# First and last RMS norm with one sum per token column, squares shared with VectorE, and the first weight group split inside that chain

## The chip, the cores and the metric

The kernel runs on one core of a Trainium2 chip. A time is the device time of one execution in microseconds (us). The engines are TensorE (PE, with its weight loads shown apart as PEld), VectorE (DVE), ScalarE (ACT), GpSimd (POOL) and SyncE (SP, which here only starts transfers). The kernel before takes 947.25 us, the median of three runs from 946.94 to 947.63.

## The reference

One trunk layer of a hybrid diffusion backbone runs on 128 context tokens and 512 latent tokens with 1024 features, in float32. What matters here are its first and last steps:

```
def rmsnorm(x, g):
    xf = x.astype(jnp.float32)
    y = xf * lax.rsqrt(jnp.mean(xf * xf, axis=-1, keepdims=True) + EPS)
    return y.astype(x.dtype) * g

h = rmsnorm(x, p['norm1_g']) * (1 + sc1) + sh1          # sub-layer 1, then the big input projection
proj = jnp.einsum('btd,dc->btc', h, p['w_in']) + p['b_in']
...                                                      # mLSTM, convolution, merge, gated MLP
y_prompt = rmsnorm(xc, final_norm_g)                     # last step
y_sample = rmsnorm(xl, final_norm_g)
```

The shift and scale (sh1, sc1) come from SiLU of a conditioning vector times a 1024 x 6144 matrix. The mLSTM, the two convolutions, the merge and the MLP between the first and the last norm are not touched by the change.

## The kernel before

Activations lie with features on the 128 partitions and the 640 tokens (128 context, 512 latent) along the columns, so x is eight tiles of 128 x 640. Every large product is made from three float32r products of a high and a low part: a weight group `wst` of eight 128 x 128 blocks is loaded, ScalarE copies it to the high part `wh`, and VectorE subtracts to get the low part `wl` (or a transfer adds it). The activations are split likewise into `hh` and `hl`.

The order of the work on each engine is the order in which the program issues it. A small planner (`_Order`) keeps an estimate of each engine's time; generators given to `od.spawn` are resumed when the estimate says that what they need is there (`od.until`), so filler work is woven into the matmul stream. It decides order only; on the chip, semaphores decide when something starts. `od.force` runs one such generator to its end at once.

**The start (lines 704 to 830).** SP starts the transfers of x[0..3], `cols` (the small per-feature constants), x[4..7], `sel` (which holds the identity `ident` and selection columns), then the conditioning matrix tiles `adst` and the first weight groups. For each x[j], ScalarE squares it (`sq`), and `colsum_into` adds it up on TensorE: four matmuls with 32 columns of ones as stationary operand, in the four column groups of the array, each streaming a quarter of the tokens (160 columns); the sums of eight tiles accumulate in one PSUM bank as 4 x 160 values, each repeated over 32 partitions. After x[3], ScalarE computes a Tanh of the conditioning vector and loads the Sqrt table. `rstd` turns the 160-column sums into the reciprocal root: a Sqrt on ScalarE, then on VectorE a scale, a reciprocal and one Newton step (three more instructions), each 160 columns wide. `bcast` spreads the result over all partitions in token order with four matmuls of 160 columns, and ScalarE copies it to `rbs`. The generator `ada1` makes the modulation: per tile j, eight float32 matmuls on `adst` (16 passes in the trace), a ScalarE copy `mrow`, two matmuls on `mrow`, then two small VectorE instructions for `mods` and `a`. `first_h(j)` multiplies x[j] by the spread factor, and makes hh and hl. Then the first projections start. A float32 matmul shows in the trace as two passes, each with its own weight load.

**The end (lines 1742 to 1790).** The last down-projections go in two token parts: `dnA` for the first TL = 384 tokens and `dnB` for the other 256. For each feature tile the residual is added on VectorE, ScalarE squares it, and VectorE adds up the squares of tiles 0 to 6 (`square_sum`); tile 7 stays apart, so there are two sums. `final(h)` then calls `sums_in` (which calls `colsum_into` twice), `rstd`, `bcast_part` (four matmuls) and the final multiply on VectorE, with a transfer out. The first part's final multiplies are woven between the second part's residuals. The middle norm uses the same helpers and keeps them.

Of the kernel before, what the change touches and what calls it, by code (L numbers as in the profile page):

```python
# [12 lines left out]
AF = mybir.ActivationFunctionType  # L13
ALU = mybir.AluOpType

P = 128
D = 1024
KD = D // P
NCTX = 128
NLAT = 512  # L20
T = NCTX + NLAT
TH = T // 2
NH = 4
NCH = T // P
# [52 lines left out]
TL = 384  # L77
# [281 lines left out]
def tile_trunk(  # L359
# [17 lines left out]
    od = _Order()  # L377
    V, S, G, PE, Q, GQ = (_Timed(e, od, k) for e, k in ((nc.vector, "V"), (nc.scalar, "S"), (nc.gpsimd, "G"),
                                                        (nc.tensor, "PE"), (nc.sync, "Q"), (nc.gpsimd, "R")))
# [19 lines left out]
    first, last = ExitStack(), ctx.enter_context(ExitStack())  # L399
    adp = first.enter_context(tc.tile_pool(name="adp", bufs=2 * NAD1))  # L400

    def A(shape, dt=F32, name="a"):
        return ap.tile(shape, dt, tag="A", name=name)
# [18 lines left out]
    def ps():  # L422
        return od.ring("ps", pools["ps"].tile([P, 512], F32, tag="ps", name="ps"), pools["nps"])
# [2 lines left out]
        return t[:, 0:T].rearrange("p (h n) -> p h n", h=2)  # L426

    HALF = [slice(0, TH), slice(TH, T)]


    cols = cp.tile([P, NCOLS], F32, name="cols")
    sel = cp.tile([P, NSEL], F32, name="sel")
    ident = sel[:, 0:128]
# [15 lines left out]
    lines = {}  # L449
# [5 lines left out]
    def load(g, must=True):  # L455
        if g in stage or g in ready or g in raws or g >= NGRP:
            return
        while len(live) >= NST:
            if not must:
                return  # L460
            od.force(next(t for t in lines.values() if not t[2]))
        t = od.ring("st", sp.tile([P, GB * P], F32, tag="st", name="wst"), NST)
        Q.dma_start(t, w_d[g])
        stage[g] = t
        live[g] = len(READS[g not in PAIRS]) if g in PAIRS or g - 1 in PAIRS else 1
# [1 line left out]
    def wtile(tag):  # L467
        return od.ring(tag, (wf[0] if tag == "wf" else wp).tile([P, GB * P], F32R, tag=tag, name=tag), CAPS[tag])

    def prep(g, tags=("wh", "wl")):  # L470


        if g in ready or g >= NGRP:
            return
        load(g)
        src = stage.pop(g)
        tag_of["c", g, 0] = tags
        hi, lo = wtile(tags[0]), wtile(tags[1])

        def parts():  # L480
            yield from od.until(src)
            S.activation(hi, src, AF.Copy)
            if g in TWICE:
                S.activation(lo, src, AF.Copy, scale=-1.0)
                live.pop(g)
                GQ.dma_start(lo, w_d[g], accum_op=ALU.add)
                return
            yield
            V.tensor_sub(lo, src, hi.bitcast(F32))
            live.pop(g)  # L490

        ready[g] = (hi, lo)
        lines[g] = od.spawn(parts())
# [137 lines left out]
    def mtile(mat, m, ks, xs, pt=None, first=True, last=True):  # L631
        pt = mm_ps() if pt is None else pt
        outs = [(bank(pt, h), HALF[h]) for h in range(2)]
        for i, k in enumerate(ks):
# [3 lines left out]
    def views(pt, t, rows=slice(0, P)):  # L638
# [3 lines left out]
        if isinstance(pt, tuple):  # L642
            return [(bank(pt, h)[rows], t[:, HALF[h]]) for h in range(2)]
        return [(pt[rows, :, 0:TH], halves(t))]
# [10 lines left out]
    ones32 = cp.tile([P, 32], F32, name="ones32")  # L655
    V.memset(ones32, 1.0)
    epsc = cp.tile([P, 1], F32, name="epsc")
    V.memset(epsc, EPS)
    bgrp = T // 4

    def colsum_into(pc, tile_, n, first, last):
        for g in range(4):
            PE.matmul(pc[32 * g:32 * g + 32, 0:n], lhsT=ones32, rhs=tile_[:, g * n:(g + 1) * n],
                      start=first, stop=last, tile_position=(0, 32 * g))

    def bcast(r, n):
        out = []
        for h in range(2):
            pt = ps()
            for j in range(2):  # L670
                g = 2 * h + j
                PE.matmul(pt[:, j * n:(j + 1) * n], lhsT=sel[:, 256 + g:257 + g].to_broadcast([P, P]), rhs=r,
                          start=True, stop=True)
            out.append(pt[:, 0:2 * n])
        return out

    def rstd(src, w, scale, name):

        y = small([P, w], name + "y")
        S.activation(y, src, AF.Sqrt, scale=scale, bias=epsc)  # L680
        v = small([P, w], name + "v")
        V.tensor_scalar(v, src, scale, EPS, op0=ALU.mult, op1=ALU.add)
        V.reciprocal(y, y)
        t = small([P, w], name + "t")
        V.tensor_mul(t, y, y)
        V.scalar_tensor_tensor(t, t, -0.5, v, op0=ALU.mult, op1=ALU.mult)
        V.scalar_tensor_tensor(y, t, 1.5, y, op0=ALU.add, op1=ALU.mult)
        return y
# [7 lines left out]
    x = []  # L696
    for j in range(KD):
        t = A([P, T], name="x")
# [21 lines left out]
    pc = ps()  # L720
    for j in range(KD):
        sq = A([P, T], name="sq")
        S.activation(sq, x[j], AF.Square)
        if j == 3:
            th = small([P, 16], "th")
            S.activation(th, colr("c"), AF.Tanh, scale=0.5)
            sqrt_table()
        colsum_into(pc, sq, bgrp, j == 0, j == KD - 1)
    V.scalar_tensor_tensor(th, th, 1.0, colr("c"), op0=ALU.add, op1=ALU.mult)
    sc_pad = cp.tile([P, KD, 32], F32, name="sc_pad")  # L730
    V.memset(sc_pad, 0.0)
# [8 lines left out]
    for nm in ("b_ua", "b_ub", "b_o", "mlstm_g", "ln_g", "ln_b", "b_ga", "b_gb"):  # L740
        a, b = _COLS[nm]
# [1 line left out]
        HC[nm] = o  # L743
        o += b - a

    r1 = rstd(pc[:, 0:bgrp], bgrp, 1.0 / D, "rs")
    prep(0)

    def hcol(name, i):
        return halfc[:, HC[name] + i:HC[name] + i + 1]  # L750
# [31 lines left out]
    def first_h(j):  # L782
        while not rbs:
            yield
        if j == 0:
            for h in range(2):
                V.tensor_mul(x[j][:, HALF[h]], x[j][:, HALF[h]], rb[h])
        else:
            V.tensor_mul(x[j], x[j], rbs[0])
        hh, hl = A([P, T], F32R, "hh"), A([P, T], F32R, "hl")  # L790
        hs.append((hh, hl))
        yield
        for c, s in ((0, slice(0, NCTX)), (1, slice(NCTX, T))):
            S.activation(hh[:, s], x[j][:, s], AF.Identity, scale=a1[:, j, c:c + 1], bias=mods[:, j, c:c + 1])
        for c, s in ((0, slice(0, NCTX)), (1, slice(NCTX, T))):
            V.tensor_scalar(x[j][:, s], x[j][:, s], a1[:, j, c:c + 1], mods[:, j, c:c + 1], op0=ALU.mult, op1=ALU.add)
        V.tensor_sub(hl, x[j], hh.bitcast(F32))
# [4 lines left out]
    t_ada = od.spawn(ada1())  # L802
    while not mrows:
        od.finish_one()
    rb = bcast(r1, bgrp)
    t = A([P, T], name="rbs")
    for h in range(2):
        S.activation(t[:, HALF[h]], rb[h], AF.Copy)
    rbs.append(t)
    pu = [mm_ps(), mm_ps()]  # L810
    pl = [ps()[:, 0:T - NFST] for _ in range(2)]
# [128 lines left out]
    for p in range(2):  # L940
        for c in range(NCH):
            t = vp.tile([P, 2, P1], F32, tag="v", name="va")
# [437 lines left out]
    for i, (nm, m) in enumerate(BRANCH):  # L1380
# [9 lines left out]
        else:  # L1390
# [4 lines left out]
            a, b = sgt.pop(("ga", m)), sgt.pop(("gb", m))  # L1395
# [33 lines left out]
    def sums_in(sums, adds, n):  # L1429

        while not all(t[2] for t in adds):
            yield
        pc = ps()
        for i in range(2):
            yield from od.until(sums[i])
            colsum_into(pc, sums[i], n, i == 0, i == 1)
        return pc[:, 0:n]

    def bcast_part(r):
        pt = ps()  # L1440
        n = r.shape[1]
        for g in range(4):
            PE.matmul(pt[:, g * n:(g + 1) * n], lhsT=sel[:, 256 + g:257 + g].to_broadcast([P, P]), rhs=r,
                      start=True, stop=True)
        return pt[:, 0:4 * n]
# [35 lines left out]
    def norm2_part(h, j, rb):  # L1481
        s = HALF[h]
        t, hh = hf[j][:, h, :], h2[j, h]
# [38 lines left out]
    for h in range(2):  # L1522
        sums, adds = [], []
        mat, s = ("woA", "woB")[h], HALF[h]
        pts = [mhalf(mat, m, range(KD - 1), mg, s, last=False) for m in range(2 if h == 0 else 0)]
        for m in range(8):
            if m < len(pts):
                pt = mhalf(mat, m, [KD - 1], mg[KD - 1:], s, pt=pts[m], first=False)
            else:
                pt = mhalf(mat, m, range(KD), mg, s)  # L1530
# [6 lines left out]
    for i in range(2):  # L1537
        t = A([P, TF], name=f"gbuf{i}")
# [200 lines left out]

    ks = LASTF  # L1740

    PARTS = [slice(0, TL), slice(TL, T)]

    def final(h, sums, adds):
        s = PARTS[h]
        n = (s.stop - s.start) // 4
        pc = yield from sums_in(sums, adds, n)
        r3 = rstd(pc, n, 1.0 / D, "rs")
        yield
        yield from od.until(r3)  # L1750
        rb = bcast_part(r3)
        if h == 0:
            for j in range(KD):
                V.scalar_tensor_tensor(x2[j][:, s], x2[j][:, s], col("final_g", j), rb, op0=ALU.mult, op1=ALU.mult)
                Q.dma_start(yT[j, :, s], x2[j][:, s])
                yield
            return
        for j in range(0, KD, 2):
            t = A([P, 2, 4 * n], name="yo")
            for i in range(2):  # L1760
                V.scalar_tensor_tensor(t[:, i, :], x2[j + i][:, s], col("final_g", j + i), rb,
                                       op0=ALU.mult, op1=ALU.mult)
            Q.dma_start(yT[j:j + 2, :, s].rearrange("j p n -> p j n"), t)
# [3 lines left out]
    for h in range(2):  # L1767
        mat, s = ("dnA", "dnB")[h], PARTS[h]
        sums, adds = [], []
        npre = NPRE if h == 0 else 0  # L1770
        pts = [dn(mhalf, mat, m, ks[:-1], s, last=False) for m in range(npre)]
        for m in range(8):
# [3 lines left out]
            if m < npre:  # L1776
                pt = dn(mhalf, mat, m, ks[-1:], s, pt=pts[m], first=False)
            else:
                pt = dn(mhalf, mat, m, ks, s)
# [136 lines left out]
```

## Time and profile before

| what | value |
| --- | --- |
| median of 3 runs (lowest, highest) | 947.25 us (946.94, 947.63) |
| the profiled execution: its time, its span | 948.37 us, 946.6 us |
| PE busy in the span | 914.1 us (97%) |
| DVE busy, ACT busy, POOL busy | 755.4 us (80%), 521.2 us (55%), 130.0 us (14%) |
| mean granted TensorE clock | 0.992 |
| chain that ended last, by engine | PE 84%, DVE 8%, ACT 4%, DMA 2%, issue 2% |

The span runs from the first to the last instruction; the execution's own time is 1.77 us longer, for what lies around it. A busy share is an average over the whole span: it says that TensorE is the engine to watch, not which engine sets the pace in the first 22 us or the last 12, where the change lies. The chain that ended last says that: it is followed back from the last instruction through whatever released each step.

### The profile page before, as it was taken

The numbers are of one execution on the slowest core, as the hardware profiler recorded it, in microseconds if no ns is written. First come the engines' busy times: TensorE is split into PE (matmuls) and PEld (weight loads), VectorE is DVE, ScalarE is ACT, GpSimd is POOL, SyncE is SP. The second block draws the span as 40 slices with busy tenths as digits, with TensorE's granted clock in tenths as the row PEclk, the third lists the DMA queues.
The fourth block names the chain that finished last, engine by engine and source line by source line (L and its number), as shares of the span: only waits on it lengthen the run. The fifth ranks groups of instructions, "written<-read, shape, count | busy, mean of one in ns | idle before, by whom it ended". The sixth has DMA issues, their size and how long they took to land.

```text
span 946.6 us, 16998 instructions
## 1 busy us (share of the span) xinstructions
PE 914.1 (97%) x6456; PEld 892.1 (94%) x6456; DVE 755.4 (80%) x1541; ACT 521.2 (55%) x994; POOL 130.0 (14%) x180
## 2 busy tenths in 40 slices
PE   5999999999999999999999989999999999999995
PEld 2899999999999999999998989999999999999995
DVE  3838989998897888888788996777778877878666
ACT  5562564267644523224689836656765666666662
POOL 0100201000000000000004313222222222222210
PEclk9999999999999999999999999999999999999998
DMA  9624939211342355576458959787888888889875
GB/s 354 263 101 80 223 79 216 73 41 61 90 134 87 126 167 200 180 268 200 155 167 186 242 152 216 166 182 165 184 170 179 177 179 176 180 177 182 205 168 150
DMA packets 65810, 158.61 MB, mean 168 GB/s; under 512 B 6848, under 2 KB 17856, under 8 KB 65728
## 3 DMA queue, kind: packets, MB, share of 16 engines
q1 hardware_dynamic: 41360, 113.20, 36.9%
q0 software_dynamic: 24368, 44.31, 28.2%
q8 instruction: 51, 0.84, 0.4%
q14 instruction: 31, 0.25, 0.1%
HBM read 142.48 MB, written 3.48 MB: 154 GB/s over the span
## 4 chain that ended last, share of the span: by engine, by line
PE 84%; DVE 8%; ACT 4%; DMA 2%; issue 2%; POOL 0%; SPq 0%; DVEq 0%; POOLq 0%; ACTq 0%
PE mm L178 64%; PE ps L178 19%; DVE acc L178 1%; DVE z L178 1%; DMA wst<-in_w 1%; DVE wl L178 1%; ACT wh L178 1%; DMA x<-in_xT 1%; DVE junk L178 1%; DMA wf<-sf 1%; DVE x L178 1%; ACT hf L178 0%; ACT L178 0%; DVE hf L178 0%; DVE bc L178 0%
## 5 line engine op out<-in xcount | busy, mean ns | idle before, releaser
L178 ACT ACTIVATE wh<-wst 128x1024 fp32r<-128x1024 f32 (+1 forms) x114 | 113.9, 1006 | 96.5 <-PE mm L178 81.9
L178 DVE SCALAR_TENSOR_TENSOR acc<-gbuf,cols,acc 128x455 f32<-128x455 f32 (+2 forms) x176 | 129.6, 739 | 16.5 <-ACT acc L178 14.0
L178 PE MATMUL mm<-hh,wh 128*128 128x320 f32 (+2 forms) x576 | 133.9, 311 | 2.5 <-ACT hh L178 1.6
L178 PE MATMUL mm<-hh,wl 128*128 128x320 f32 (+2 forms) x576 | 134.0, 312 | 0.2 <-DVE wl L178 0.2
L178 PE MATMUL mm<-hl,wh 128*128 128x320 f32 (+2 forms) x576 | 133.3, 310 | 0.0
L178 DVE SCALAR_TENSOR_TENSOR z<-glu,cols,z 128x641 f32<-128x641 f32 (+14 forms) x120 | 102.4, 888 | 6.3 <-ACT z L178 5.5
L178 DVE TENSOR_TENSOR wl<-wst,wh 128x1024 fp32r<-128x1024 f32 x72 | 87.6, 1220 | 19.7 <-ACT wh L178 19.3
L178 PEld LDWEIGHTS mm<-hh,wh 128*128 128x128 f32 x576 | 96.7, 188 | 4.6 <-ACT hh L178 2.1
L178 PEld LDWEIGHTS mm<-hl,wh 128*128 128x128 f32 x576 | 96.5, 188 | 1.8 <-issue 1.3
L178 PEld LDWEIGHTS mm<-hh,wl 128*128 128x128 f32 x576 | 96.3, 188 | 1.4 <-issue 0.7
L178 PE MATMUL mm<-h,wh 128*128 128x320 f32 x452 | 85.7, 310 | 2.3 <-ACT h L178 1.3
L178 PE MATMUL mm<-ah,wh 128*128 128x320 f32 (+2 forms) x336 | 81.1, 311 | 5.2 <-DVE x L178 5.2
L178 DVE SCALAR_TENSOR_TENSOR junk<-ad,cb 128x512 bf16<-128x512 f32 x128 | 82.1, 685 | 0.0
L178 PE MATMUL mm<-al,wh 128*128 128x320 f32 (+2 forms) x336 | 80.9, 310 | 0.0
L178 PE MATMUL mm<-ah,wl 128*128 128x320 f32 (+2 forms) x336 | 80.8, 310 | 0.0
L178 PEld LDWEIGHTS mm<-h,wh 128*128 128x128 f32 x452 | 71.1, 188 | 4.0 <-ACT h L178 1.6
L178 PE MATMUL mm<-h,wl 128*128 128x320 f32 x364 | 73.1, 309 | 0.0
L178 DVE SCALAR_TENSOR_TENSOR x<-mm,mods,x 128x128 f32<-128x128 f32 (+1 forms) x168 | 63.7, 432 | 7.2 <-PE mm L178 6.6
L178 POOL DMA_DIRECT2D wl<-in_w x52 | 45.1, 868 | 144.1 <-ACT wl L178 65.9
L178 PEld LDWEIGHTS mm<-ah,wh 128*128 128x128 f32 x336 | 57.7, 189 | 5.6 <-issue 5.4
L178 ACT ACTIVATE wl<-wst 128x512 fp32r<-128x512 f32 (+1 forms) x74 | 56.4, 792 | 4.7 <-PE mm L178 4.7
L178 PEld LDWEIGHTS mm<-h,wl 128*128 128x128 f32 x364 | 58.4, 188 | 0.1
(250 smaller groups left out, 1944.6 us busy)
## 6 DMA issues: line engine op xcount, KB each, us to landing
wst<-in_w SPq DMA_DIRECT2D x138, 512.0 KB, 4.5
ad<-in_ada SPq DMA_DIRECT2D x64, 256.0 KB, 3.3
wl<-in_w POOLq DMA_DIRECT2D x30, 512.0 KB, 7.4
adst<-in_ada SPq DMA_DIRECT2D x16, 512.0 KB, 10.2
wf<-in_w POOLq DMA_DIRECT2D x23, 256.0 KB, 5.4
wh<-sf POOLq DMA_DIRECT2D x22, 256.0 KB, 5.1
wl<-in_w POOLq DMA_DIRECT2D x22, 256.0 KB, 6.1
x<-in_xT SPq DMA_DIRECT2D x16, 320.0 KB, 5.2
```

The lines of the kernel that those rows point to most:

```text
L178: return fn(*args, **kw)
```

## The change

Both outer norms take their sums in another shape. In `token_sums` the squared tile is the stationary operand (128 tokens at a time) and one column of ones is streamed, so that the sum of token p of chunk c lands on partition p, column c: five matmuls of one column for 640 tokens. `rstd` then works on 5 columns at the start, and on 3 and 2 at the end. `token_rows` spreads the result: the column of a chunk, repeated 128 times, is the stationary operand and the identity is streamed. In the start, VectorE squares x[3], x[4], x[5] and x[7], the Tanh and the Sqrt table follow x[2], and the first weight group is split right after the first `mrow`, ahead of the spread, without the planner's wait for its landing. The first norm's parts are now 384 and 256 tokens instead of 320 and 320. The new functions are whole in the diff.

```
-    def prep(g, tags=("wh", "wl")):
+    def prep(g, tags=("wh", "wl"), wait=True):
...
         def parts():
-            yield from od.until(src)
+            if wait:
+                yield from od.until(src)
             S.activation(hi, src, AF.Copy)
...
+    def token_sums(pc, tile_, w, first, last):
+
+        n = w // P
+        for c in range(n):
+            PE.matmul(pc[:, c:c + 1], lhsT=tile_[:, c * P:(c + 1) * P], rhs=ones32[:, 0:1], start=first and c == 0,
+                      stop=last and c == n - 1)
+
+    def token_rows(r, a, b):
+
+        pt = ps()
+        for c in range(a, b):
+            PE.matmul(pt[:, (c - a) * P:(c - a + 1) * P], lhsT=r[:, c:c + 1].to_broadcast([P, P]), rhs=ident,
+                      start=True, stop=True)
+        return pt[:, 0:(b - a) * P]
...
         sq = A([P, T], name="sq")
-        S.activation(sq, x[j], AF.Square)
-        if j == 3:
+        if j in (3, 4, 5, 7):
+            V.tensor_mul(sq, x[j], x[j])
+        else:
+            S.activation(sq, x[j], AF.Square)
+        if j == 2:
...
-        colsum_into(pc, sq, bgrp, j == 0, j == KD - 1)
+        token_sums(pc, sq, T, j == 0, j == KD - 1)
...
-    r1 = rstd(pc[:, 0:bgrp], bgrp, 1.0 / D, "rs")
-    prep(0)
+    r1 = rstd(pc[:, 0:NCH], NCH, 1.0 / D, "rs")
...
             for h in range(2):
-                V.tensor_mul(x[j][:, HALF[h]], x[j][:, HALF[h]], rb[h])
+                V.tensor_mul(x[j][:, PARTS[h]], x[j][:, PARTS[h]], rb[h])
...
-    rb = bcast(r1, bgrp)
+    prep(0, wait=False)
+    od.force(lines[0])
+    rb = [token_rows(r1, 0, 3), token_rows(r1, 3, NCH)]
...
     def final(h, sums, adds):
         s = PARTS[h]
-        n = (s.stop - s.start) // 4
-        pc = yield from sums_in(sums, adds, n)
-        r3 = rstd(pc, n, 1.0 / D, "rs")
+        n = (s.stop - s.start) // P
+        while not all(t[2] for t in adds[:-1]):
+            yield
+        yield from od.until(sums[0])
+        pc = ps()
+        token_sums(pc, sums[0], n * P, True, False)
+        while not adds[-1][2]:
+            yield
+        yield from od.until(sums[1])
+        token_sums(pc, sums[1], n * P, False, True)
+        r3 = rstd(pc[:, 0:n], n, 1.0 / D, "rs")
         yield
         yield from od.until(r3)
-        rb = bcast_part(r3)
+        rb = token_rows(r3, 0, n)
...
```

## Rows read from the trace of the kernel before

**Rows 1.** The chain that ended last, start of the kernel: start us, length us, what.

```profile
10.52 2.69 PE ps L178 x32
...
16.17 4.35 PE ps L178 x28
...
20.93 1.09 ACT hh L178 x2
...
22.06 0.56 PE mm L178 x2
```

**Rows 2.** Busy time by engine in a stretch, after the start.

```profile
22.00:40.00 18.00, 17.94 (x167) 14.13 (x168) 14.73 (x33) 8.74 (x18) 3.47 (x17) 1.00 0.89 354
```

**Rows 3.** The chain that ended last, end of the kernel.

```profile
934.89 0.41 DVE x L178
...
935.79 0.36 PE ps L178 x8
...
936.17 0.32 ACT rsy L178
...
938.13 1.96 PE ps L178 x8
```

**Rows 4.** Timeline of PE in the start: start us, us, operation.

```profile
4.35 0.76 PE L178 MATMUL ps<-sq,ones 128*32 128x160 f32 x8 [4.35 <-ACT sq L178]
...
18.46 1.01 PE L178 MATMUL ps<-sel,mrow 128*128 128x128 f32 x4
...
19.41 1.07 PE L178 MATMUL ps<-adst,sc_pad 128*32 128x256 f32 x16
...
22.46 0.61 PE L178 MATMUL ps<-sel,mrow 128*128 128x128 f32 x4
```

**Rows 5.** PE groups by form: count, busy us, mean ns of one, idle before.

```profile
L178 PE MATMUL ps<-rsy,sel 128*128 128x64 f32 x8 | 1.9, 424 | 2.0 <-DVE rsy L178 2.0
```

**Rows 6.** Issues on SP, and time to landing of x[7] and of the first wst.

```profile
3.08 2.43 SPq L178 DMA_DIRECT2D x<-in_xT  x4
...
DMA to landing us min/median/max: 6.6/6.6/6.6
...
8.10 0.33 SPq L178 DMA_DIRECT2D wst<-in_w  x1
...
DMA to landing us min/median/max: 7.4/7.4/7.4
```

**Rows 7.** Stretches after PE idled from 563.5 to 568.7; last columns: clock, DMA.

```profile
571.00:572.00 1.00, 1.00 (x6) 1.00 (x5) 0.58 (x1) 1.00 (x3) 0.04 (x1) 0.50 0.82 319
572.00:573.00 1.00, 1.00 (x8) 1.00 (x7) 0.78 (x2) 1.00 (x3) 0.83 (x1) 0.87 0.94 348
```

**Rows 8.** Timeline of DVE and ACT between the sums and the first projection.

```profile
13.90 1.14 DVE L178 RECIPROCAL rsy<-rsy 128x160 f32<-128x160 f32 x1
...
15.79 0.32 DVE L178 SCALAR_TENSOR_TENSOR rsy<-rst,rsy 128x160 f32<-128x160 f32 x1
...
19.04 1.05 ACT L178 ACTIVATE wh<-wst 128x1024 fp32r<-128x1024 f32 x1
...
19.84 0.87 DVE L178 TENSOR_TENSOR x<-x,ps 128x320 f32<-128x320 f32 x2
...
20.63 1.22 DVE L178 TENSOR_TENSOR wl<-wst,wh 128x1024 fp32r<-128x1024 f32 x1
```

**Rows 9.** Timeline of DVE in the last norm.

```profile
936.66 0.54 DVE L178 RECIPROCAL rsy<-rsy 128x64 f32<-128x64 f32 x1
...
937.76 0.23 DVE L178 SCALAR_TENSOR_TENSOR rsy<-rst,rsy 128x64 f32<-128x64 f32 x1
```

**Rows 10.** Timeline of PE near the end, first part's sums and spread, last product.

```profile
922.70 0.54 PE L178 MATMUL ps<-sq,ones 128*32 128x96 f32 x16
...
926.66 1.13 PE L178 MATMUL ps<-rsy,sel 128*128 128x96 f32 x8
...
933.85 0.28 PE L178 MATMUL mm<-ah,wl 128*128 128x256 f32 x1
```

More of the change, by code (lines that the diff above doesn't have):

```diff
@@ L428, in tile_trunk @@
     HALF = [slice(0, TH), slice(TH, T)]
+    PARTS = [slice(0, TL), slice(TL, T)]
     cols = cp.tile([P, NCOLS], F32, name="cols")
@@ L658, in tile_trunk @@
     V.memset(epsc, EPS)
-    bgrp = T // 4
     def colsum_into(pc, tile_, n, first, last):
@@ L804, in tile_trunk @@
         od.finish_one()
-    rb = bcast(r1, bgrp)
+    prep(0, wait=False)
+    od.force(lines[0])
+    rb = [token_rows(r1, 0, 3), token_rows(r1, 3, NCH)]
     t = A([P, T], name="rbs")
     for h in range(2):
-        S.activation(t[:, HALF[h]], rb[h], AF.Copy)
+        S.activation(t[:, PARTS[h]], rb[h], AF.Copy)
     rbs.append(t)
@@ L1740, in tile_trunk @@
     ks = LASTF
-    PARTS = [slice(0, TL), slice(TL, T)]
     def final(h, sums, adds):
         s = PARTS[h]
-        n = (s.stop - s.start) // 4
-        pc = yield from sums_in(sums, adds, n)
-        r3 = rstd(pc, n, 1.0 / D, "rs")
+        n = (s.stop - s.start) // P
[9 more added lines that the diff above has]
+        r3 = rstd(pc[:, 0:n], n, 1.0 / D, "rs")
         yield
         yield from od.until(r3)
-        rb = bcast_part(r3)
+        rb = token_rows(r3, 0, n)
         if h == 0:
@@ L1758, in final @@
         for j in range(0, KD, 2):
-            t = A([P, 2, 4 * n], name="yo")
+            t = A([P, 2, n * P], name="yo")
             for i in range(2):
```

## The prediction

> **What bounds the kernel now.** I read four views: the chain that ended last, at both ends of the span; busy time by stretch; the timeline of each engine in the first 24 us and the last 25; and the groups by form, for prices. The reader is to see three things.
>
> First, from the first projection on, TensorE is the pace: it starts at 22.06 [rows 1] and in 22 to 40 us it is busy 17.94 of 18 us [rows 2]. So what the change does to the start counts by one number, the moment of that first projection; whatever moves it moves the rest.
>
> Second, before 22.06 the chain is a latency path: column sums end at 13.21, the 160-column reciprocal root runs on ScalarE and VectorE until the spread starts at 16.17, TensorE spreads and makes the first modulation until 20.52, then hh at 20.93 and the projection [rows 1]. TensorE runs at half speed here, whatever the clock column says of it: the same four passes on `mrow` take 1.01 us at 18.46 and 0.61 us at 22.46 [rows 4].
>
> Third, after the last product (933.85 [rows 10]) the end is a latency path again: a VectorE residual that starts late (934.89), sums at 935.79, root from 936.17, spread from 938.13 to 940.09 [rows 3], then eight final multiplies and the transfers.
>
> **The change part by part.** *The price of a pass.* The new sums stream one column, a form the trace does not have. What it has is a pass with few columns against a full 128-column weight load: eight passes of 64 columns at half clock took 1.96 us [rows 3], with 424 ns for one [rows 5], so (1.96 - 0.424)/7 = 0.22 us from start to start. Streaming 64 columns cannot be the limit, since four passes of 128 columns take 0.61 us at full clock [rows 4] and 1.01 at half, hardly more per pass; the weight load is. So a one-column pass costs about 0.22 us at half clock and 0.11 at full. Its lower bound is the load of 32 columns in `colsum_into`, a quarter of that; I take the full load, because the new stationary operand is 128 columns wide.
>
> The Trainium skill (TensorE: Matmul & The Clock Gate, section "LDWEIGHTS (loading the stationary operand)") gives the load as columns over 1.2 GHz whatever the clock, an estimate of 0.107 us for 128. At full clock the trace agrees, at half clock the 0.22 us does not. By that rule the sums would never fall behind; what this would give is rival C below.
>
> *Sums at the start.* One tile costs ten passes: 2.2 us at half clock, 1.1 at full, against 0.625 us per tile before (four tiles from 10.52 to 13.21 with the drain [rows 1]). They start at 4.35 as before [rows 4]. x[7] is issued at about 4.7 and lands 6.6 us later, at 11.3 [rows 6]; a VectorE square of 640 columns takes about 0.85 us (two halves of 320 took 0.87 [rows 8]), so the last square is there at 12.2, hardly earlier than the 12.35 at which ScalarE was done before. The squares on VectorE therefore buy nearly nothing: TensorE becomes the queue. All at half clock the sums would end at 4.35 + 8 x 2.2 = 21.9; all at full clock at 12.2 + 1.1 = 13.3.
>
> Which of these holds hangs on when the clock rises. Twice the trace shows the rise: after 568.7, when matmuls ran without a gap, half speed lasted until the stretch 572 to 573, some 3.6 us [rows 7]; and in the start the spread began at 16.17, the passes at 18.46 were still slow, and those at 19.41 fast [rows 4], some 3.2 us. In the new order TensorE has work without a gap from 5.5 us on, since each tile costs more than the squares' spacing. I take the rise at 9.4, 5 us after the first pass, since the sums begin with gaps: 2.3 tiles before it, 5.7 x 1.1 = 6.3 us after, end at 15.7. A rise 2 us to either side gives 14.7 and 16.7 as bounds. That is 2.5 us later than 13.21.
>
> *Root, spread, split.* An instruction of the Newton step takes 0.32 us at 160 columns and 0.23 at 64, so about 0.17 at 5; the reciprocal 1.14 and 0.54, so about 0.17 [rows 8, 9]. With a Sqrt of some 0.26 (0.32 at 64 columns [rows 3]) the root takes 0.26 + 0.16 + 0.15 + 3 x 0.19 + gaps = 1.25 us instead of the 2.9 between 13.21 and 16.17. Meanwhile TensorE does the sixteen `adst` passes (1.07 at full clock [rows 4]), which hides most of it. Call the end of the sums E. `mrow` is copied by E + 1.5, the first weight group is split on ScalarE (1.05) and VectorE (1.22 [rows 8]) by E + 3.8. The spread (ten passes) runs from E + 1.3 to E + 2.5, the `mrow` passes end at E + 3.0. On VectorE the weight split is now queued ahead of the small `mods` and `a` instructions and of the multiply of x[0], so those wait until E + 3.8, 0.8 us longer than needed; then 0.45 for `mods` and `a`, 0.87 for x [rows 8], 1.1 for hh [rows 1], with gaps: first projection at E + 6.35. With E = 15.7 that is 22.05, against 22.06: nothing, with bounds of 1 us either way. The late sums eat what the short root, the full-speed spread and the early split save.
>
> *The end.* First part: sixteen column-sum passes (0.47 us to the next product) and eight spread passes (0.88 us, plus some 0.2 of waiting for the root) [rows 10] become twelve and six passes of 0.11, 1.98 us: 0.43 later for TensorE. On VectorE the shorter root frees about 1 us and lets the first part's final multiplies start a good 1 us sooner, so the last residual no longer starts 0.7 us behind the last product [rows 3, 10]: 0.6 earlier, if the queue really clears; nothing at the lower bound. Last sums: four passes and a drain, 0.6 instead of 0.36. Root: 1.1 instead of 1.82 us (936.17 to 937.99). Spread: four passes instead of eight narrower ones; 0.65 at full clock, 1.1 at half, I take 0.9, against 2.1 with the issue gap before it. Together +0.43 - 0.6 + 0.24 - 0.7 - 1.2 = -1.8 us, bounds -0.9 and -2.3. Nothing hides this: each step is alone on the chain, and the final multiplies follow at once.
>
> *Sum.* 948.37 - 1.8 = 946.6 for the profiled execution, which lies 1.12 above the median; against the median 945.4.
>
> **The rivals.** *A, the clock stays low through the sums.* No row shows one-column passes raise it, and the start already has work that did not: column sums without a gap from 10.52 to 13.21 [rows 1], then `adst` passes, yet the passes at 18.46 are slow [rows 4]. Against it: that work uses 32-column loads, the new one full ones. Then E = 21.9, the `adst` passes and the spread run slowly too (about 1.6 us more on the path), and the first projection comes at about 29.9, 7.8 us later; with the end's gain 947.25 + 7.8 - 1.8 = 953.3, slower. It decides as soon as the rise comes later than about 14 us.
>
> *B, a late rise*, in the middle of the sums at 12 to 14 us: E near 18, a start 2.3 us later, the end as above: 947.7, no change that can be told.
>
> *C, the load costs no more at half clock than at full*, 0.11 us (the rule above): the sums keep up, E = 13.3. The weight group, landing at 8.1 + 7.4 = 15.5 [rows 6], then holds the split, and the first projection comes near 20.4: 1.7 earlier, 943.7 in all. The 0.22 us speaks against it.
>
> **How the numbers follow.** The forecast has 0.46 (945.4, own range 944.2 to 946.5), A 0.30, B 0.14, C 0.10. A measurement of this kernel tells about 0.2%, 1.9 us, from no change. The forecast lies on that line: half of it is faster, half the same. Faster: 0.23 + 0.10, and a little for a larger gain at the end, 0.35. Same: 0.23 + 0.10, 0.33. Slower: A and the late side of B, 0.32. The range runs from C's 943.5 up into A, to 953.2, which leaves out about half of A and little else.
>
> **What would show it.** Right: the sums' one-column passes spaced 0.22 us at first and 0.11 later, the last one near 15.7; the first projection within 1 us of 22; the span from the last product to the first final multiply (934.1 to 940.1 now) shorter by about 2 us; the spread at the end four passes. Wrong: one-column passes spaced far below 0.11 us (then the queue on TensorE never forms); slow passes beyond 14 us (A); a last residual that still starts 0.7 us behind the last product (the end gains only 1 us); or a change anywhere between 22 and 900 us, where this working has none.

## The result, and the profile after

The changed kernel takes 956.07 us, median of 4 runs (954.93 to 956.61), against 947.10 for the kernel before beside it (946.69 to 947.63). The ratio is 1.0086, with a 95% interval of 1.0074 to 1.0098: slower by about 8 us by the ratio (the two medians lie 9.0 apart), where 945.4 was forecast. It is rival A, and somewhat more. The profiled execution after took 954.93 us, with a span of 953.2.

The start, first the chain that ended last (start us, length us, what), then the timeline of TensorE (PE), both of the kernel after:

```profile
4.57 22.72 PE ps L178 x126
...
27.69 1.09 ACT hh L178 x2
```

```profile
4.57 17.23 PE L178 MATMUL ps<-ones,sq 128*128 128x1 f32 x80 [4.57 <-ACT sq L178]
21.72 1.93 PE L178 MATMUL ps<-adst,sc_pad 128*32 128x256 f32 x16
23.59 2.21 PE L178 MATMUL ps<-sel,rsy 128*128 128x128 f32 x10
25.63 0.61 PE L178 MATMUL ps<-sel,mrow 128*128 128x128 f32 x4
26.17 1.07 PE L178 MATMUL ps<-adst,sc_pad 128*32 128x256 f32 x16
28.82 0.56 PE L178 MATMUL mm<-hh,wh 128*128 128x256 f32 x2 [1.59 <-ACT hh L178]
```

The reader is to see that one engine now holds the start: 126 passes of TensorE follow each other from 4.57 to 27.29, where before the chain went through squares, the long root and the spread [rows 1]. The 80 one-column passes take 17.15 us to the next one's start, 0.214 us each, from the first to the last. The `adst` passes behind them take 1.93 us, where the next sixteen, at 26.17, take 1.07; the four `mrow` passes at 25.63 take 0.61, the full-speed price [rows 4]. So the clock was at half until about 25, not until 9.4. The first projection comes at 28.82, against 22.06.

Busy time of the weight-load side of TensorE (PEld) in the same start: stretch, its length, busy us (count of loads), clock column, DMA share, GB/s:

```profile
8.00:12.00 4.00, 4.00 (x21) 1.00 1.04 413
12.00:16.00 4.00, 4.00 (x20) 1.00 0.99 393
```

The load side is busy all the time, as forecast, and five loads a microsecond is all it does. The clock column cannot be used here: it shows 1.00 until the first change that is on record, while the rate of the passes shows half speed.

The end, the chain of the kernel after:

```profile
943.15 0.41 DVE x L178
...
944.05 0.62 PE ps L178 x4
...
944.70 0.27 ACT rsy L178
...
945.65 0.17 DVE rsy L178
...
945.96 0.70 PE ps L178 x4
...
946.67 0.48 DVE yo L178
```

The last product starts at 942.16. From there to the first final multiply is 4.5 us, where the spread's end was 6.2 us behind it before [rows 3, 10]: the root takes 1.12 us from its Sqrt to its last step (1.82 before) and the spread 0.70 (1.96). The residual still starts 0.99 us behind that start (1.04 before).

For the whole way, moments in the profiled executions, in us of the span (the sums' end is the last column sum's; "weights 1" is the last product of the first weight-group stage, `ps<-hh,wl`; "va" the first product `ps<-va,kw`; "hAh" and "h" the first products on those tiles). The experiments below stand in the same table.

| kernel | sums end | first projection | weights 1 | va | hAh | h | last product ends | span |
|---|---|---|---|---|---|---|---|---|
| before | 13.2 | 22.06 | 60.70 | 121.86 | 275.85 | 482.42 | 934.13 | 946.6 |
| after | 21.8 | 28.82 | 67.57 | 129.00 | 283.54 | 490.61 | 942.44 | 953.2 |
| e1 end only | 13.0 | 20.39 | 59.03 | 122.53 | 276.52 | 483.11 | 935.37 | 946.3 |
| e2 start only | 21.9 | 30.18 | 68.92 | 131.72 | 286.31 | 493.37 | 945.04 | 956.8 |
| e4 warm | 21.8 | 29.35 | 68.10 | 130.61 | 285.18 | 492.25 | 944.74 | 956.0 |
| e5 wide | 15.7 | 21.39 | 60.17 | 123.00 | 277.54 | 484.72 | 937.87 | 949.1 |
| e6 old start, filled | 15.1 | 22.48 | 61.12 | 123.90 | 277.88 | 484.48 | 937.12 | 948.1 |
| e7 wide, late split | 17.2 | 22.48 | 62.71 | 125.66 | 279.79 | 486.81 | 939.42 | 950.1 |
| e8 wide, late split, filled | 14.5 | 19.77 | 61.25 | 123.82 | 277.94 | 484.97 | 937.21 | 947.9 |
| e9 squares only | 13.1 | 21.49 | 62.89 | 127.07 | 280.92 | 487.40 | 939.40 | 951.1 |
| e10 old start, early split | 13.6 | 22.54 | 61.14 | 122.69 | 276.77 | 483.37 | 935.63 | 946.9 |
| e11 the same, filled | 13.3 | 20.72 | 59.57 | 121.36 | 275.43 | 482.02 | 935.25 | 946.3 |
| e12 wide, split, filled | 14.6 | 21.28 | 60.07 | 120.70 | 275.27 | 482.48 | 934.66 | 945.9 |

After less before: +6.87 at the end of weights 1, +1.44 more by the last product (+0.27 by va, +0.55 by hAh, +0.50 by h, +0.12 behind it), -1.75 from there to the end of the span: +6.56. The medians differ by 9.0, because this profiled execution of after was the lowest of its four and that of before lay 1.3 above the median beside it.

### The profile page after: what moved, and what is told of

The parts are those of the page before. It is cut to its first block, busy times and chain, and to the rows that moved or that the text cites. A ratio compares the mean times of both kernels' runs of the same rounds, so it can differ in the third digit from the quotient of the medians.

```text
span 953.2 us, 16996 instructions
## 1 busy us (share of the span) xinstructions
PE 925.6 (97%) x6456; PEld 908.7 (95%) x6456; DVE 756.1 (79%) x1545; ACT 518.4 (54%) x990; POOL 130.0 (14%) x180
## 4 chain that ended last, share of the span: by engine, by line
PE 86%; DMA 4%; DVE 4%; ACT 3%; issue 2%; POOL 0%; SPq 0%; DVEq 0%; POOLq 0%; ACTq 0%
PE mm L178 65%; PE ps L178 21%; DMA wst<-in_w 1%; DMA E<-in_mask 1%; DMA wl<-in_w 1%; DVE wl L178 1%; ACT wh L178 1%; DVE junk L178 1%; DMA wf<-sf 0%; DVE acc L178 0%; ACT hf L178 0%; DMA E<-rowM 0%; DMA x<-in_xT 0%; DVE bc L178 0%; DVE yo L178 0%
## 5 line engine op out<-in xcount | busy, mean ns | idle before, releaser
L178 DVE SCALAR_TENSOR_TENSOR acc<-gbuf,cols,acc 128x455 f32<-128x455 f32 (+2 forms) x176 | 129.8, 740 | 16.9 <-ACT acc L178 14.5
```

Source lines behind the costliest of these rows:

```text
L178: return fn(*args, **kw)
```

## The experiments

Ratios are to the kernel before on the same chip, with 95% intervals. That kernel took 950.6 us beside e1 to e5, 950.8 beside e6 to e9 and 949.2 beside e10 to e12 (medians of 25 to 30 runs); these are three chips. There is no profile of it from them, so moments in traces are held against the one profile of before.

### e1 and e2: one end at a time

e1 is the kernel before with the new sums, root and spread in the last norm alone:

```diff
-        pc = yield from sums_in(sums, adds, n)
-        r3 = rstd(pc, n, 1.0 / D, "rs")
...
+        token_sums(pc, sums[0], n * P, True, False)
...
+        token_sums(pc, sums[1], n * P, False, True)
+        r3 = rstd(pc[:, 0:n], n, 1.0 / D, "rs")
...
-        rb = bcast_part(r3)
+        rb = token_rows(r3, 0, n)
```

> The new last norm with the old first norm; the order of all work before the end is that of the kernel before. Theory 1 (the loss is the start, where sums queue behind weight loads at half clock; the end gains as forecast): 947.1 - 1.75 = 945.4 us, first projection at 22.06, from the last product to the span's end 10.7 us instead of 12.5. Rival theory 2 (the end is what loses, or gains nothing): 947 us or more.

Measured: 0.9992 (0.9979 to 1.0004). The time does not show a gain; it allows one of up to 2.0 us. The trace shows one at the end (below), but of another size than forecast.

e2 is the reverse, the new start with the old end.

> The new first norm with the old last norm. Theory 1: slower than the changed kernel by the end's gain, 956.1 + 1.75 = 957.8 us; first projection near 28.8; the stretch from first projection to last product about 913.6 us. Theory 2: no slower than the changed kernel, 956 us.

Measured: 1.0081 (1.0064 to 1.0099), first projection at 30.18. The start alone makes the loss. TensorE in the start of e2:

```profile
4.67 17.23 PE L178 MATMUL ps<-ones,sq 128*128 128x1 f32 x80 [4.67 <-ACT sq L178]
21.83 1.93 PE L178 MATMUL ps<-adst,sc_pad 128*32 128x256 f32 x16
23.70 2.50 PE L178 MATMUL ps<-sel,rsy 128*128 128x128 f32 x10
25.99 1.06 PE L178 MATMUL ps<-sel,mrow 128*128 128x128 f32 x4
```

The sums take the same 17.23 us as in the kernel after; the spread is 0.3 us slower and the `mrow` passes are at half speed too, since the clock rose later still. That moment differs from execution to execution.

### e5: the same loads, 96 streamed columns

The one edit against the kernel after is the width of the streamed operand of the start's sums; stationary operands, their order and their count stay, and the root reads one of each 96 equal columns.

```diff
-            PE.matmul(pc[:, c:c + 1], lhsT=tile_[:, c * P:(c + 1) * P], rhs=ones32[:, 0:1], start=first and c == 0,
...
+            lhsT, rhs = tile_[:, c * P:(c + 1) * P], ones32[:, 0:1]
...
+            nc.tensor.matmul(pc[:, c * wide:(c + 1) * wide], lhsT=lhsT,
+                             rhs=rhs.to_broadcast([P, wide]) if wide > 1 else rhs, start=first and c == 0,
...
-        token_sums(pc, sq, T, j == 0, j == KD - 1)
+        token_sums(pc, sq, T, j == 0, j == KD - 1, 96)
```

> The changed kernel with 96 columns of ones streamed in the first norm's sums instead of one; the weight loads, the instruction count and the order of all work are the same, and one of each 96 equal columns is used. At half clock 96 columns still stream in less time than a 128-column weight load takes. Theory 1: streamed columns raise the clock, so the passes go from 0.214 to 0.11 us some 3 to 7 us after the first, the sums end at 14.7 to 16.7 us instead of 21.7, the first projection is near 22 to 23 us, the kernel takes 948 to 950 us. Rival theory 3 (a set time) and rival theory 4 (loads of squared tiles are slow in themselves): the same as the changed kernel, sums end at 21.7, 956 us.

Measured: 1.0017 (1.0005 to 1.0030). Its loads (PEld) by stretch, and its chain:

```profile
4.00:8.00 4.00, 3.49 (x17) 1.00 0.99 335
8.00:10.00 2.00, 2.00 (x17) 1.00 1.03 396
10.00:12.00 2.00, 2.00 (x20) 1.00 1.04 407
12.00:15.00 3.00, 3.00 (x29) 1.00 1.03 401
```

```profile
4.51 11.17 PE ps L684 x80
...
16.92 2.87 PE ps L178 x30
```

The passes run at five a microsecond until 8, and at ten from about 9 on. The sums end at 15.67, where the forecast had 15.7. With 96 times the columns, the passes are never slower than with one, so the load is what a pass costs, and its price here goes with the clock. The loads being the same, it was the streamed columns that brought the clock up here. The loads are not slow in themselves, nor did the clock wait for a set time.

### e4: raise the clock first

The kernel after, with four products of 512 columns on constants ahead of the sums:

```diff
+    for _ in range(4):
+        nc.tensor.matmul(warm, lhsT=ones32[:, 0:1].to_broadcast([P, P]), rhs=ones32[:, 0:1].to_broadcast([P, 512]),
+                         start=True, stop=True)
```

> The changed kernel with four float32 products of 512 columns on ones, results unused, issued on TensorE ahead of the first sums; they take about 7 us at half clock. Theory 1 (the clock is low because one-column passes do not raise it): the clock rises during these products and the first sums run at 0.11 us a pass; if one-column passes also hold it up, the 80 passes end near 15.3 us and the kernel takes some 950 us; if they let it fall, the first 25 to 40 passes are fast and the rest slow, the sums end near 20 us and the kernel takes some 954 us. Rival theory 3 (the clock rises at a set time after the start, near 19 to 25 us, whatever TensorE does): every pass takes 0.214 us, the sums end near 25 us, the kernel takes some 959 us.

Measured: 1.0051 (1.0034 to 1.0067). The wide products and the sums on TensorE, and then its loads by stretch, in which the column behind the count is the granted clock:

```profile
0.95 6.15 PE L738 MATMUL ps<-ones 128*128 128x512 f32 x8 [0.95 <-DVE epsc L178]
6.95 14.89 PE L178 MATMUL ps<-ones,sq 128*128 128x1 f32 x80
```

```profile
7.00:8.00 1.00, 1.00 (x10) 1.00 1.04 409
8.00:9.00 1.00, 1.00 (x11) 1.00 1.03 406
9.00:10.00 1.00, 1.00 (x8) 0.67 1.03 408
10.00:11.00 1.00, 1.00 (x7) 0.50 1.09 422
...
24.00:26.00 2.00, 2.00 (x11) 0.50 1.03 412
```

This is the clearest view of the case. The clock was at full when the one-column passes began, they ran ten a microsecond, and in the stretch from 9 to 10 the clock fell under them, although the load side was busy for the whole of each stretch. It stayed at half until after 26. So in this start such passes neither raised the clock (after, e2) nor held it (e4). The profiled execution took 957.7 us, one of the four longest of ten; the others took 953.2 to 955.3, so the sums may have ended earlier in them.

### e9: the squares alone

The kernel before with the squares of tiles 3, 4, 5 and 7 on VectorE, and the Tanh behind the third square.

> The kernel before with one edit alone: VectorE squares tiles 3, 4, 5 and 7, and the Tanh comes behind the third square. Theory (the landing of x[7] sets the last square, so it buys nearly nothing): sums end within 0.3 us of 13.21, time within 0.2% of before. Rival: ScalarE's squares were the limit, sums end 0.6 us or more earlier and the first projection with them.

Measured: 1.0039 (1.0021 to 1.0058), slower by 3.7 us, which no theory had. The sums end at 13.1, as forecast: the squares buy 0.1 us. What is lost comes later. TensorE around the first projection, and its stretches (all engines; the column behind POOL's is the clock):

```profile
21.49 0.56 PE L178 MATMUL mm<-hh,wh 128*128 128x256 f32 x2 [2.14 <-ACT hh L178]
21.98 1.44 PE L178 MATMUL ps<-adst,sc_pad 128*32 128x256 f32 x16
23.35 0.90 PE L178 MATMUL mm<-hl,wh 128*128 128x256 f32 x2
24.05 1.07 PE L178 MATMUL ps<-sel,mrow 128*128 128x128 f32 x4
```

```profile
22.00:23.00 1.00, 1.00 (x17) 0.39 (x16) 0.97 (x2) 0.00 (x0) 0.00 (x0) 0.77 1.02 410
23.00:24.00 1.00, 1.00 (x6) 0.60 (x3) 0.30 (x1) 0.38 (x1) 0.59 (x1) 0.50 1.01 401
24.00:25.00 1.00, 1.00 (x5) 0.83 (x4) 0.00 (x0) 0.00 (x0) 0.68 (x9) 0.50 1.03 410
```

Two things follow from an order that the planner now writes otherwise. The second group of 16 `adst` passes, which stood in TensorE's idle time ahead of the first projection [rows 4], stands behind it, so 1.1 us of work moves into the stretch where TensorE is the pace; and the idle time ahead of the projection grows to 2.14 us, after which the clock falls to half in 22 to 26. Ahead of va TensorE idles another 2.02 us, until 117.1, and the clock is at 0.50 again in 119 to 121. By the end of weights 1 this kernel is 2.2 us behind before, although its projection began 0.6 us earlier. In the kernel after the `adst` group stands ahead (26.17) and the idle time is 1.59, so this loss is not part of the result; it shows that the moment of the first projection alone is not the measure that the prediction took it for.

### e7: when the weight group is split

The wide version with the weight group's split at its old place:

```diff
     r1 = rstd(pc[:, 0:96 * NCH:96], NCH, 1.0 / D, "rs")
+    prep(0)
...
-    prep(0, wait=False)
-    od.force(lines[0])
```

> The version with 96 streamed columns in the start's sums, but the first weight group split at its old place, behind the small multiplies. Prices the early split: as the prediction had it, the split on VectorE (1.22 us) stands ahead of the modulation's small instructions and holds them; theory: first projection 0.5 to 0.8 us earlier than with the early split, near 20.8 instead of 21.39. Rival: the split is late now and holds the first projection, which stays at 21.4 or comes later. If the order of later work is what costs the 3 us that the wide version lies above its two ends' gains, the time should fall by 1 to 3 us with it too (the later order is then nearer to that of before).

Measured: 1.0008 (0.9995 to 1.0020). The clock rose later here than in e5 (ten passes a microsecond from 12 on), so moments are counted from the sums' end. The first projection comes 5.3 us behind it instead of 5.7: the early split does hold the small multiplies, as the prediction said, by less than its 0.8. But the last product of weights 1 comes 45.5 us behind instead of 44.5: `wl` now stands between the first multiplies and `hl`, and the second `adst` group again runs behind the first projection. By these two profiles the early split is worth about 1 us to this start. VectorE in e7:

```profile
20.65 0.88 DVE L178 TENSOR_TENSOR x<-x,ps 128x384 f32<-128x384 f32 x2
21.45 1.22 DVE L178 TENSOR_TENSOR wl<-wst,wh 128x1024 fp32r<-128x1024 f32 x1
...
23.41 0.83 DVE L178 TENSOR_TENSOR hl<-x,hh 128x640 fp32r<-128x640 f32 x1
```

From the end of weights 1 to the end of the last product it takes 876.7 us instead of 877.7, the least that was expected. Of that, va to hAh gives 0.4 and hAh to h 0.2; 0.5 lies behind h, where e4 and e5, which do the same work there, differ by 0.7 too.

### e10: the early split on the old start

```diff
-    prep(0)
...
     rb = bcast(r1, T // 4)
+    prep(0, wait=False)
+    od.force(lines[0])
```

> Old start (32-column-load sums, ScalarE squares, long root) and new end, with one part of the new start: the first weight group split right behind the spread instead of after the first multiplies. Theory (the early split is worth about 1 us, since the lower half of the weights no longer stands between the first multiplies and the lower half of x): the first projection stays within 0.5 us of where the old start has it for the same moment of the clock's rise, the last product of the first weight-group phase (60.70 before, 59.03 in the old start with the new end) comes about 1 us earlier, and the time is 1 to 2 us below before with the end. If the early split is also what costs later (0.55 us between the attention's first products and the next projection, which the versions with it show and those without do not), that stretch is 0.55 us longer here too. Rival: the split ahead of the small multiplies delays the first projection by 0.8 us and nothing comes back.

Measured: 0.9998 (0.9985 to 1.0011). From the sums' end to the last product of weights 1 it takes 47.6 us, at a rise of the clock that is 0.6 us later than in before, and 47.5 in before: no gain that can be told. In before, `wl` also stands between the first multiplies and `hl` [rows 8], but nothing waits for it: `hl` is there at 23.46, and TensorE has `mrow` and `adst` passes to do until 24.00. The stretch va to hAh is 154.1 us here, 154.0 in before and 154.5 in after and e5: the early split by itself is not what costs there.

### e6, e8, e11, e12: constant products to fill TensorE's idle time

Constant products (outputs unused) in TensorE's idle time, to have a full clock: in the gaps of the old sums (e6), ahead of the wide sums (e8, with the late split), between the `adst` passes and the old spread (e11, on e10), and ahead of the wide sums and of the first projection (e12, on e5).

```diff
+    fill_pe(2, 512)                      # e6, e8, e12: ahead of the sums
...
+        if j < KD - 1:
+            fill_pe(1, 128)              # e6: behind each tile's sums
...
+    fill_pe(1, 320)                      # e11: ahead of the spread (e6: 256)
...
+        if j == 0:
+            fill_pe(1, 384)              # e12: ahead of the first projection
```

> Old start (four 32-column-load sums per tile, ScalarE squares, the short root of the new form left out) with the new end, and products of constants put into the gaps of the old sums: two of 512 columns first, one of 128 behind each of the first seven tiles' sums, one of 256 ahead of the spread. They add nothing to the output. Theory (wide passes raise the clock, loads with one streamed column do not): the clock is at full from before the sums' end, the spread and the adst passes run at 0.11 us per pass instead of 0.22, the first projection starts near 20.3 instead of 22.06, and with the end's -1.75 the time is some 3 us below before. Rival: the fillers delay the sums as much as the clock gives back; first projection at 22 or later, time -1.75 or less below before.

> The late-split version with 96 streamed columns, and two products of 512 columns on constants ahead of the sums (outputs unused). Theory: clock at full before the second tile's sums, so they follow the squares as these come; sums end at 14 to 14.8, first projection near 20, time some 3 us below before (start -2, end -1.75, less what the later order costs). Rival: the sums end is set by the last square and the weight group's landing at 15.5, so the first projection stays within 0.4 us of the version without the products.

> The kernel with old sums, early split and new end, and one product of 320 columns of constants in the idle time of TensorE between the adst passes and the spread (output unused). Theory: the filler and the adst passes together raise the clock by about 17, so most of the spread runs at full speed: the spread with the mrow passes takes about 2 instead of 3.2 us, first projection 0.8 to 1.2 us earlier than a rise at 19.3 gives (22.06 before). Rival: the clock rises in this start by 14.3 to 19.3 by itself, at random, so the filler changes nothing that a time shows.

> The new start with 96 streamed columns and its early split, two products of 512 columns of constants ahead of the sums, and one of 384 in TensorE's idle time ahead of the first projection (outputs unused). Theory: sums at full clock from their second tile, end near 14.5; no fall of the clock behind the idle time (the late-split version with products ahead had it at half from 20.9 to 24.3); first projection near 20.2, last product of the first weight-group phase near 59.0 (60.70 before); end -1.0; the later order costs +1.0; time 1.5 to 2.5 us below before. Rival: the weight group's landing at 15.5 and the split ahead of the small multiplies hold the first projection at 21 or later, and the time equals that of before.

Measured: e6 0.9991 (0.9981 to 1.0002), e8 1.0003 (0.9990 to 1.0016), e11 0.9994 (0.9982 to 1.0005), e12 0.9997 (0.9984 to 1.0011). None beats the kernel before by what can be told. e6's rival held: the sums end at 15.1. The clock, at full from about 6, was lost again under fillers of 128 columns and sums of 160, with no idle time above 1.35 us, and the last sums ran at half speed:

```profile
12.00:13.00 1.00, 1.00 (x14) 0.72 1.03 422
13.00:14.00 1.00, 1.00 (x10) 0.50 1.01 414
```

So passes of that width with gaps between them did not hold it here. e8 has the earliest projection of all, 19.77, and loses it at once: 2.19 us of idle time ahead of it, the `adst` group behind it, and a clock at half from 20.9 to 24.3, as in e9. In e11 the spread is fast and the projection at 20.72, but that is not the filler's work: it starts at 15.04, and the eight `adst` passes ahead of it, from 14.47, already take 0.64 us where the first eight took 0.94. e1, with no filler, had 20.39: the old start finds a full clock by itself now and then. e12 did what was forecast of its sums (14.6) and of its clock, but its first projection is at 21.28 and its time that of before, the outcome that its rival had, in the main for another reason: the second `adst` group comes 0.99 us late, behind a wait in which the chain shows nothing that was waited for, and ScalarE's copy of it stands ahead of hh:

```profile
17.03 0.61 PE L178 MATMUL ps<-sel,mrow 128*128 128x128 f32 x4
18.63 1.07 PE L178 MATMUL ps<-adst,sc_pad 128*32 128x256 f32 x16 [0.99 <-PE ps L178]
19.63 0.91 PE L743 MATMUL ps<-ones 128*128 128x384 f32 x2
21.28 0.56 PE L178 MATMUL mm<-hh,wh 128*128 128x256 f32 x2 [0.74 <-ACT hh L178]
```

A gain in the start also has a second gate behind it, the landing of the attention mask ahead of va. The chain of e1 there (in before it goes through VectorE's `z`):

```profile
96.93 3.79 DMA E<-rowM
100.72 9.90 DMA E<-in_mask
...
114.06 8.56 PE mm L178 x66
```

e1 is 1.7 us ahead of before's profile at the end of weights 1 and 0.7 behind at va, with the same instructions in between: the mask takes 12.6 us from issue to landing instead of 11.8 and its rows 13.0 instead of 11.2, and TensorE idles 2.8 us instead of 1.0 in 85 to 122. Between the same two points e1 to e8 are 1.4 to 2.3 us slower than before's profile, with either start, e9, with its second fall of the clock, 3.0 and e10 to e12, on a third chip, -0.5 to 0.6; after, timed beside before, is 0.3 slower. Most of it seems to be the chip and not the change; without a profile of before from those chips that is not shown.

## Why the prediction was wrong

**The step that failed** is one sentence: "In the new order TensorE has work without a gap from 5.5 us on ... I take the rise at 9.4". The first half came true and the second doesn't follow from it. TensorE had work without a gap, its load side busy for 4.00 of every 4.00 us, and the clock stayed at half until it had streamed the `adst` passes and the first spread passes. e5 shows that the streamed columns were missing, e4 that work of this kind lets a full clock fall. The two rises that the prediction read [rows 4, 7] were both behind passes that stream 128 to 320 columns; the one counter-example in the trace, the sums without a gap from 10.52 [rows 1], it put down to the 32-column loads.

The Trainium skill (TensorE: Matmul & The Clock Gate, "Part 1: The HAM clock gate") puts it as "activity releases the throttle" and does not tell loading from streaming. Here 17 us of passes with a busy load side released nothing; the 96-column passes with the same loads did.

**The size of it.** The sums end 6.1 us later than forecast (21.8 against 15.7), and from there to the first projection it takes 7.0 us, not 6.35, since the `adst` passes and most of the spread run at half speed too. Together 28.82 instead of 22.05. That is A's working to within 1.1 us (29.9), and e2 has 30.18.

**What was right at the start.** The price of a pass: 0.214 us at half and ten a microsecond at full clock, for 0.22 and 0.11. The Trainium skill (TensorE: Matmul & The Clock Gate, "LDWEIGHTS (loading the stationary operand)") gives one price for the load, columns over 1.2 GHz, with no word on the clock. At half clock e4 speaks against it, where loads of one form run at ten a microsecond and then at five in one trace; rival C fell with that. The root took 1.15 us (21.83 to 22.99 in after) for 1.25. The split does stand ahead of the small multiplies (`wl` at 25.08 for 1.22, `mods` at 26.27), but the 0.8 us that it was to cost them is too much: the `mrow` passes that they also need end at 26.24 here, and in e5 at 18.75 with `mods` at 19.24. The squares on VectorE buy nothing at the sums' end (e9). With the rise about where the prediction had it (between 8 and 9 us), e5's first projection is at 21.39, 0.7 better than the sum.

**The end** looks right, -1.75 from the last product to the end for -1.8 forecast, and isn't. The last spread on TensorE, in the old form and in the new, each at two moments of the clock (before's row of the old form at half is in [rows 3]); e2 and e9:

```profile
948.99 1.30 PE L178 MATMUL ps<-rsy,sel 128*128 128x64 f32 x8 [2.02 <-DVE rsy L178]
```

```profile
943.37 1.24 PE L178 MATMUL ps<-rsy,sel 128*128 128x64 f32 x8 [2.02 <-DVE rsy L178]
```

and after and e5:

```profile
945.96 0.68 PE L178 MATMUL ps<-sel,rsy 128*128 128x128 f32 x4 [1.30 <-DVE rsy L178]
```

```profile
941.39 1.19 PE L178 MATMUL ps<-sel,rsy 128*128 128x128 f32 x4 [1.30 <-DVE rsy L178]
```

The old spread takes 1.96 or 1.24 to 1.30 us, the new one 1.19 or 0.68, as the clock has fallen before the spread or not. Before's profile had the one and after's the other. In e2 and e9 the clock fell under the last two of the eight passes (275 ns for one, then 422), so the old form wholly at full clock is not on record and would be shorter still. From the last product's start to the end it is 12.75 and 12.02 to 12.06 us in the old form, 11.50 to 11.52 and 11.00 in the new (e1, e6 and e11, where it fell during the spread, lie between): the end gains 1.25 with both at half clock, and at most 1.0 to 1.05 with both at full. Of that, twelve one-column passes in the first part (1.39 us for 0.54) take back 0.1 to 0.3 ahead of the last product, where the forecast had 0.43 (from the first `mm<-ah,wf` to its end 27.46 to 27.51 us with the new end, 27.23 to 27.36 with the old), which leaves about 1.0 at half clock and at most 0.9 at full, near the forecast's lower bound. The terms that were mis-sized: the residual (-0.6; it starts 0.9 to 1.0 us behind the last product's start in every kernel, the queue on VectorE doesn't clear), and the spread (-1.2 with its issue gap; the passes gained 0.8 at half clock and less than 0.6 at full). Sums (+0.24) and root (-0.7) came as forecast. A gain of 0.9 is a ratio of 0.9991; e1 measured 0.9992, though its interval includes no gain.

**The middle**, for which the prediction had nothing, costs 1.4. From hAh to h, the kernel after and the six of the experiments that have the new sums in the start (with 1 or 96 columns, and with the new root and spread) take 207.0 to 207.2 us, and the six with the old ones, before among them, 206.5 to 206.6: 0.4 to 0.7 us in every one, whatever the clock at the start or the end. From va to hAh it is 0.55 us more where the new sums and the early split come together (after, e2, e4, e5, e12), 0.1 with the new sums and the late split (e7, e8), and at most 0.1 with the early split on old sums (e10, e11). Between va and h it is neither a wait nor the other order of later work that the expectations of e7 to e12 speak of. TensorE, VectorE and ScalarE do the same instructions, by the names and shapes of their tiles, in the same order from va to h, before and after, and TensorE idles as long; its busy time is what grows. TensorE in before, then in after (stretch, its length, busy us, count, clock, DMA share, GB/s):

```profile
121.86:275.85 153.99, 153.66 (x1130) 1.00 0.36 100
275.85:482.42 206.57, 205.57 (x1459) 1.00 0.52 171
```

```profile
129.00:283.54 154.54, 154.22 (x1130) 1.00 0.36 100
283.54:490.61 207.07, 206.06 (x1459) 1.00 0.52 171
```

The difference builds up over nearly the whole way, some 0.4 ns per product, and no single one is more than 31 ns later. What makes the same products slower was not settled.

**The sum again**, in the steps of the prediction: start +6.8 for 0, middle +1.4 for 0 (with 0.1 more by weights 1), end -1.75 for -1.8, of which 0.5 to 0.7 is the moment of the clock's fall. e1's and e2's ratios multiply to 1.0073, and with their intervals to 1.0043 to 1.0103, which holds the 1.0086: the two ends add up, as far as the times can tell. The medians' difference, 9.0 us, is larger than the profiles' 6.6. Within one form of the sums the start's end also moves with the moment of the rise: 20.39, 22.06 and 22.54 with the old ones (e1, before, e10), 28.82 and 30.18 with the new ones (after, e2).

## What to carry to other kernels

Ask of a stretch that is to bring TensorE's clock up what it streams, not only whether it is busy: here passes with a full stationary load and one streamed column left the clock at half for 17 us, and let a full clock fall within 3 us, where the same loads with 96 columns reached the full one. Where a single profile shows a gain at an end with the clock in play, look at the clock in both before believing it; here 0.5 to 0.7 of 1.75 us was that. And judge a start by a point some tens of us behind it: twice an earlier first projection was gone by the end of the first weight-group stage.

## What the runs showed that had not been expected

Under one-column passes with a busy load side the granted clock fell from 1.00 to 0.50 (e4, between 9 and 10 us). It also fell to 0.50 behind idle times of TensorE of 2.14 us (e9, until 26), 2.02 us (e9 again, until after 121) and 2.19 us (e8, until 24), and did not behind 2.19 us in e7 or 2.30 us in e1. In e6 it fell with no idle time above 1.35 us. With 96 streamed columns instead of one, a pass with a full load took no longer at either clock (ten a microsecond, and five). And the same instructions in the same order took TensorE 1.05 us longer from va to h with the new start (359.2 and 360.3 us busy).
